# A decoder layer's start reordered, four unread matmuls added, and the last stage's loads, stores and final rows rewritten

## The chip, the cores and the metric

One core of a Trainium2 chip runs the whole program. The metric is the device time of one execution in microseconds. Engines are called as in the profile: PE (matmul), PEld (its weight loads), DVE, ACT, POOL, and the DMA queues of SP and POOL.

## The reference

The layer takes x (2048 x 1024, float32). Cut to what matters:

```python
h = rms_norm(x, pre_g)
q, k, v, g_ret, u, g_pool = split(h @ w_in, 6)            # 1024 -> 6 x 1024
y_ret = group_norm(retention(rope(q), rope(k), v)) * silu(g_ret)   # 8 heads, chunks of 128
y_pool = pooling(u, pool_w) * silu(g_pool)                # windows 2, 4, 8, 16
y = concat([y_ret, y_pool]) @ w_out                       # 2048 -> 1024
return x + rms_norm(y, post_g)
```

The rotary tables are the sine and cosine of position times inverse frequency.

## The kernel before

**The matmuls.** Every float32 matmul is made of three passes: both operands are split into a high part (ACT, `split`, L144) and a rest (DVE, L145), and high by high, high by rest and rest by high are accumulated (L330 to L332). The projections are done for pairs of 512-row blocks by Strassen's scheme in Winograd's form. A `Unit` has four quadrants, 11, 12, 21 and 22, of 128 x 512, and seven products of twelve matmuls each, in the order 6, 2, 5, 7, 1, 4, 3, where product 1 is that of the next unit. The scheme needs sums of quadrants: S1 = 21 + 22 and S3 = 11 + 21 are made while loading (`land`, L261 a plain load on SP's queue, then L263 a second load on POOL's queue that adds to the tile), S2 = S1 + 11 and S4 = S2 + 12 on DVE (L281). Four PSUM banks of the tag `acc` hold products; DVE takes results out of them (L313, L340, L348, L354, L693).

**The stages.** `first()` (written in a fixed order, which `manual_schedule` keeps) makes the statistics of x for blocks 0 and 1 and the first head without Strassen. Then four phases of units follow: mixer units of blocks 0 and 1, of blocks 2 and 3, and two of output units, eight each, over the two halves of the 2048 channels. In the phases a planner orders each engine's instructions; `later(i, f)` puts f into the i-th next slot, of which there is one per product.

**The start.** SP's queue issues row tile 0 of x (128 x 1024), the constants `cst`, the positions, row tiles 1 to 3, the gains `col`, then transposed x and weights. ACT squares each row tile in place with a sum (L862); DVE works out angles from the positions (`angles`, eight instructions at L835), six of them while it waits for the rows; then mean and inverse root (L370, L134 to L139), a diagonal (L376), which PE spreads over partitions (`rb`, L384), the rests of two weight tiles (L878) and the last two angle steps. The loop over `made((s11, s21))` is the first block: in each of eight rounds DVE scales a tile by `rb` (L932) and makes its rest (L940), ACT its high part (L936), DVE in most rounds the rest of a weight tile (L878), and PE does six matmuls (L951 to L953). The second block (k index 2 and 3) uses the same tiles, the third is the first one's for block 1, the fourth the second's; in the second DVE does block 1's angles and statistics and the rotary multiplications.

**The last phase.** Each of its eight output units adds the other phase's partial sums (`parts`, loaded at L687 into tiles of the tag `t`, of which there are 16), takes squares on ACT (L697) and then, in `finish`, an inverse root on DVE, four multiplications with the scale and the gain `pg` (L723), four DMAs on POOL's queue that add x to the tiles (L729), and four slots later four stores on SP's queue (L733). The very last unit (`final`) does each row when its two quadrants are there: x loaded at L722, multiplied at L723, three of four additions on POOL and one on DVE (L727), stored at L731.

Of the kernel before, what the change touches and what calls it, by code (L numbers as in the profile page):

```python
# [81 lines left out]
def layer_kernel(ctx: ExitStack, tc: tile.TileContext, x, xt, pos, wt, wut, wo, pw, cols, postg, const, out):  # L82
# [14 lines left out]
    cst = kp.tile([P, C_W], F32, name="cst")  # L97
    col = kp.tile([P, 3 * KT], F32, name="col")
# [153 lines left out]
    class Unit:  # L252
        def __init__(self, name, quads, uses):
            self.name, self.quads, self.uses = name, quads, uses
            self.op, self.bank = {}, {}
            self.fetch = self.part = None

# [8 lines left out]
        def load_sums(self):  # L266
            self.raw = {}
            self.land("S1", "21", "22")
            self.land("S3", "11", "21")

        def load_rest(self, names):
            for q in names:
                self.land(q, q)
# [15 lines left out]
        def prep(self, i):  # L289
            raw = self.raw  # L290
            if i == 1:
                h11 = raw["11"]
                self.split(1, "11")
                self.add("S2", raw["S1"], h11, nc.vector)
            elif i == 2:
                self.add("S4", raw["S2"], raw["12"], nc.vector)
                self.split(6, "S2")
            elif i == 3:
                self.split(2, "12")
            elif i == 4:  # L300
# [361 lines left out]
    def out_unit(s, f0, last, final=False):  # L662
# [21 lines left out]
        def fetch():  # L684
            for q in ("11", "22", "21", "12"):
                parts[q] = T(f"pt{q}_{n}")[:, :BLK]
                nc.sync.dma_start(out=parts[q], in_=place(part, q))  # L687

        def total(q):
            def use(c, i):  # L690
                t = o[q] = T(f"ot{q}_{n}")[:, :BLK]
                if i:
                    nc.vector.tensor_tensor(out=t, in0=c, in1=parts[q], op=ALU.add)  # L693
                else:
                    c(t)
                k = 2 * (int(q[0]) - 1) + int(q[1]) - 1
                nc.scalar.activation(out=parts[q], in_=t, func=AF.Square, scale=1.0 / 32.0,  # L697
                                     accum_out=s2[:, k:k + 1])
                if final and q == "21":
                    finish(("22", "21"))  # L700
                elif final and q == "12":
                    finish(("11", "12"))
                elif q == "12":
                    later(2, lambda: finish(("11", "22", "21", "12")))
            return use

        def finish(quads):
            k0, nr = int(quads[0][0]) - 1, len(quads) // 2
            rows_s = slice(0, 2) if nr == 2 else slice(k0, k0 + 1)
            v = sml.tile([P, nr], F32, name=f"ov{n}{k0}", tag=f"ov{nr}")  # L710
            s3 = s2.rearrange("p (s j) -> p s j", j=2)
            nc.vector.scalar_tensor_tensor(out=v, in0=s3[:, rows_s, 0], scalar=EPS, in1=s3[:, rows_s, 1],
                                           op0=ALU.add, op1=ALU.add)
            rs = rsqrt(v, nr, f"f{n}{k0}")
            for q in quads:
                k, j = (int(q[0]) - 1 if nr == 2 else 0), int(q[1]) - 1
                t = o[q]
                row = rows[q[0]]
                spot = (slice(row * P, (row + 1) * P), slice(j * BLK, (j + 1) * BLK))
                if final:  # L720
                    xr = T(f"xr{q}_{n}")[:, :BLK]
                    nc.sync.dma_start(out=xr, in_=x[spot])  # L722
                nc.vector.scalar_tensor_tensor(out=t, in0=t, scalar=rs[:, k:k + 1], in1=pg[j],  # L723
                                               op0=ALU.mult, op1=ALU.mult)
                if final:
                    eng = nc.vector if q == "12" else nc.gpsimd
                    eng.tensor_tensor(out=t, in0=t, in1=xr, op=ALU.add)  # L727
                else:
                    nc.gpsimd.dma_start(out=t, in_=x[spot], accum_op=ALU.add)  # L729
                if final:  # L730
                    nc.sync.dma_start(out=out[spot], in_=t)  # L731
                else:
                    later(4, lambda t=t, spot=spot: nc.sync.dma_start(out=out[spot], in_=t))  # L733

        u = Unit(n, quads, {q: total(q) for q in quads})
        u.fetch, u.part = fetch, parts
# [106 lines left out]
    def first():  # L843
# [63 lines left out]
        load_w(1, 0)  # L907
        load(b11[1], xt[0, 1])
# [90 lines left out]
        for i in made((s11, s21)):  # L999
# [9 lines left out]
            if i == 2:  # L1009
                trig(0)  # L1010
# [173 lines left out]
```

## Time and profile before

| | us |
|---|---|
| median of 3 runs | 1480.18 (1474.72 to 1480.51) |
| profiled execution, its own time | 1476.45 |
| span of the profile | 1474.5 |
| PE busy | 1423.2 (97%) |

The span runs from the first to the last instruction of the profiled execution. Times in rows are microseconds from its start.

### The profile page before, as it was taken

The page shows a single profiled execution, that of the slowest core. Times are in us where ns is not written, and L with a number is a line of the kernel's source. Part 1 is how long each engine was busy: PE and PEld are TensorE (multiplying, and loading weights), DVE is VectorE, ACT ScalarE, POOL GpSimd, SP SyncE. Part 2 cuts the span into 40 slices and gives each one's busy share as a digit, 9 for nine tenths or more (in the row PEclk, how much of TensorE's full clock was granted, in tenths as well). Part 3 has the DMA queues.
Part 4 walks back from the last instruction along what each step waited for, and adds up shares of the span by engine and source line. Part 5 has one row for each costly group of instructions (what it writes and reads, how often), then busy time and mean ns, then how long its engine had stood idle before and what let it go on. Part 6 is the DMA issues. An engine that isn't in the chain of part 4 may idle for free. (4 is left out here: it accounts for less than half of the span.)

```text
span 1474.5 us, 20756 instructions
## 1 busy us (share of the span) xinstructions
PE 1423.2 (97%) x6976; PEld 1188.4 (81%) x6976; DVE 1085.0 (74%) x2360; ACT 712.3 (48%) x1353; POOL 249.1 (17%) x335
## 2 busy tenths in 40 slices
PE   5999999999999999999999999999999999998985
PEld 3788888888888888888888888888888788877764
DVE  7997677878867788967787868687778544676665
ACT  6464565545554545745444444454446433553321
POOL 0001010211111222110111112111111222202222
PEclk9999999999999999999999999999999999999998
DMA  9135365635363768743535536444638755789976
GB/s 341 30 92 135 89 174 149 189 102 154 111 172 100 235 202 240 244 108 94 151 115 153 160 101 171 127 153 134 168 92 268 216 153 152 229 273 227 235 209 164
DMA packets 115370, 243.77 MB, mean 165 GB/s; under 512 B 14016, under 2 KB 14144, under 8 KB 115264
## 3 DMA queue, kind: packets, MB, share of 16 engines
q1 hardware_dynamic: 79296, 156.46, 32.1%
q0 software_dynamic: 35968, 86.00, 25.8%
q8 instruction: 54, 0.88, 0.3%
q14 instruction: 52, 0.43, 0.1%
HBM read 187.88 MB, written 54.53 MB: 164 GB/s over the span
## 5 line engine op out<-in xcount | busy, mean ns | idle before, releaser
L330 PE MATMUL b_o<-rh,h_o 128*128 128x512 f32 x192 | 76.3, 398 | 11.6 <-DVE ot_o L348 11.6
L331 PE MATMUL b_o<-rl,h_o 128*128 128x512 f32 x192 | 76.1, 396 | 0.7 <-DVE rl L145 0.7
L332 PE MATMUL b_o<-rh,l_o 128*128 128x512 f32 x192 | 76.0, 396 | 0.0
L330 PE MATMUL b_up<-rh,h_up 128*128 128x512 f32 x192 | 75.5, 393 | 0.0
L450 POOL DMA_DIRECT2D yd<-sg x32 | 24.1, 753 | 304.0 <-DVE sg L531 226.3
L332 PE MATMUL b_up<-rh,l_up 128*128 128x512 f32 x192 | 74.8, 390 | 0.0
L331 PE MATMUL b_up<-rl,h_up 128*128 128x512 f32 x192 | 74.8, 389 | 0.0
L330 PE MATMUL b_vg<-rh,h_vg 128*128 128x512 f32 x180 | 72.0, 400 | 0.0
L330 PE MATMUL b_qk<-rh,h_qk 128*128 128x512 f32 x180 | 71.2, 396 | 0.0
L332 PE MATMUL b_qk<-rh,l_qk 128*128 128x512 f32 x180 | 70.3, 391 | 0.1
L332 PE MATMUL b_vg<-rh,l_vg 128*128 128x512 f32 x180 | 70.4, 391 | 0.0
L331 PE MATMUL b_vg<-rl,h_vg 128*128 128x512 f32 x180 | 70.2, 390 | 0.0
L331 PE MATMUL b_qk<-rl,h_qk 128*128 128x512 f32 x180 | 70.2, 390 | 0.0
L524 ACT ACTIVATE on<-op,sh,y_o 128x128 f32<-128x128 f32 x128 | 48.2, 457 | 36.9 <-DVE sh L521 36.9
L145 DVE TENSOR_TENSOR rl<-m,rh 128x1024 fp32r<-128x1024 f32 x42 | 51.1, 1223 | 19.6 <-ACT rh L144 15.5
L263 POOL DMA_DIRECT2D S_qk<-in_wt x30 | 26.4, 907 | 170.4 <-DMA S_qk<-in_wt 119.3
L330 PEld LDWEIGHTS b_o<-rh,h_o 128*128 128x128 f32 x192 | 36.6, 191 | 21.6 <-DVE ot_o L348 13.6
L330 PE MATMUL a_o<-rh,h_o 128*128 128x512 f32 x128 | 49.9, 390 | 2.6 <-ACT x_o L338 2.6
L144 ACT CAST rh<-m 128x1024 fp32r<-128x1024 f32 x42 | 43.7, 1048 | 15.7 <-DMA m<-made 8.4
L330 PE MATMUL c_o<-rh,h_o 128*128 128x512 f32 x128 | 50.3, 393 | 0.8 <-ACT rh L144 0.8
L331 PE MATMUL c_o<-rl,h_o 128*128 128x512 f32 x128 | 50.1, 392 | 0.3 <-DVE rl L145 0.3
L332 PE MATMUL c_o<-rh,l_o 128*128 128x512 f32 x128 | 49.8, 389 | 0.0
(498 smaller groups left out, 4552.8 us busy)
## 6 DMA issues: line engine op xcount, KB each, us to landing
m<-made SPq DMA_DIRECT2D x30, 512.0 KB, 6.2
made<-c POOLq DMA_DIRECT2D x48, 256.0 KB, 3.8
yd<-sg POOLq DMA_DIRECT2D x32, 256.0 KB, 2.7
S_up<-in_wt POOLq DMA_DIRECT2D x32, 256.0 KB, 5.7
yd<-mx POOLq DMA_DIRECT2D x32, 256.0 KB, 3.1
b<-in_wo SPq DMA_DIRECT2D x32, 256.0 KB, 4.5
S_o<-yd SPq DMA_DIRECT2D x32, 256.0 KB, 3.0
S_o<-yd POOLq DMA_DIRECT2D x32, 256.0 KB, 7.5
```

The source lines that it names most:

```text
L144: nc.scalar.copy(out=r32(hi), in_=val)
L145: (eng or nc.vector).tensor_tensor(out=r32(lo), in0=val, in1=hi, op=ALU.subtract)
L263: nc.gpsimd.dma_start(out=dst, in_=self.quads[more], accum_op=ALU.add)
L330: nc.tensor.matmul(o, wh, mh, start=opens and j == 0, stop=False, **more)
L331: nc.tensor.matmul(o, wh, ml, start=False, stop=False, **more)
L332: nc.tensor.matmul(o, wl, mh, start=False, stop=j == KH - 1, **more)
L450: nc.gpsimd.dma_start(out=yd[b][:, :, f, :], in_=t.rearrange("p (c t) -> p c t", c=CPB))
L524: nc.scalar.activation(out=self.on[:, c], in_=op[:, c], func=AF.Identity, scale=rs[:, i:i + 1], bias=shift[:, i:i + 1])
```

## The change

At the start all four row tiles are loaded first, then `cst`, which now holds the gains as well (one DMA less); the positions come after the first weights. Four matmuls of `ones` with half a squared row tile each write a PSUM tile that nothing reads: three follow the squares of row tiles 0 to 2, the fourth stands behind `rb` on PE. The eight angle steps move: one behind the weight rests, six into the rounds 2 to 7 of the first block, one behind it. The rotary tables' sine and cosine (`trig(0)`, ACT) move from round 2 to behind the squares of block 1.

In the last phase the units are `plain`: quadrants 21 and 22 are loaded as they are, and S1 and S3 are made on DVE, two additions per unit, in place of three more loads, two of which add. `finish` begins one slot earlier and is spread over two slots; the stores go to POOL's queue, two slots after the DMA that adds x. In the final unit x is loaded together with the partial sums, each quadrant is multiplied by the gain as it arrives, and one DVE instruction per quadrant scales it and adds x.

```diff
-    cst = kp.tile([P, C_W], F32, name="cst")
-    col = kp.tile([P, 3 * KT], F32, name="col")
+    cst = kp.tile([P, C_W + 3 * KT], F32, name="cst")
+    col = cst[:, C_W:]
...
@@ Unit
         def load_sums(self):
             self.raw = {}
+            if self.plain:
+                self.land("21", "21")
+                self.land("22", "22")
+                return
             self.land("S1", "21", "22")
             self.land("S3", "11", "21")
 
         def load_rest(self, names):
             for q in names:
-                self.land(q, q)
+                if q not in self.raw:
+                    self.land(q, q)
...
         def prep(self, i):
             raw = self.raw
-            if i == 1:
+            if i == 0 and self.plain:
+                self.add("S1", raw["21"], raw["22"], nc.vector)
+            elif i == 1:
                 h11 = raw["11"]
+                if self.plain:
+                    self.add("S3", raw.pop("21"), h11, nc.vector)
                 self.split(1, "11")
                 self.add("S2", raw["S1"], h11, nc.vector)
...
@@ out_unit
             for q in ("11", "22", "21", "12"):
                 parts[q] = T(f"pt{q}_{n}")[:, :BLK]
                 nc.sync.dma_start(out=parts[q], in_=place(part, q))
+            if final:
+                for q in ("22", "21", "12", "11"):
+                    xr[q] = T(f"xr{q}_{n}")[:, :BLK]
+                    nc.sync.dma_start(out=xr[q], in_=x[spot(q)])
...
-                if final and q == "21":
-                    finish(("22", "21"))
-                elif final and q == "12":
-                    finish(("11", "12"))
+                if final:
+                    nc.vector.tensor_tensor(out=t, in0=t, in1=pg[int(q[1]) - 1], op=ALU.mult)
+                    if q in ("21", "12"):
+                        row = q[0]
+                        rs = scales(int(row) - 1, 1)
+                        for e in (row + "2", row + "1") if row == "1" else (row + "1", row + "2"):
+                            nc.vector.scalar_tensor_tensor(out=o[e], in0=o[e], scalar=rs, in1=xr[e],
+                                                           op0=ALU.mult, op1=ALU.add)
+                            nc.sync.dma_start(out=out[spot(e)], in_=o[e])
                 elif q == "12":
-                    later(2, lambda: finish(("11", "22", "21", "12")))
+                    later(1, finish)
...
+        def finish():
+            rs = scales(0, 2)
+
+            def normed(q):
+                k, t = int(q[0]) - 1, o[q]
                 nc.vector.scalar_tensor_tensor(out=t, in0=t, scalar=rs[:, k:k + 1], in1=pg[int(q[1]) - 1],
                                                op0=ALU.mult, op1=ALU.mult)
-                if final:
-                    eng = nc.vector if q == "12" else nc.gpsimd
-                    eng.tensor_tensor(out=t, in0=t, in1=xr, op=ALU.add)
-                else:
-                    nc.gpsimd.dma_start(out=t, in_=x[spot], accum_op=ALU.add)
-                if final:
-                    nc.sync.dma_start(out=out[spot], in_=t)
-                else:
-                    later(4, lambda t=t, spot=spot: nc.sync.dma_start(out=out[spot], in_=t))
+                nc.gpsimd.dma_start(out=t, in_=x[spot(q)], accum_op=ALU.add)
+                later(2, lambda: nc.gpsimd.dma_start(out=out[spot(q)], in_=t))
+            for i, q in enumerate(("11", "22", "21", "12")):
+                later(i // 2, lambda q=q: normed(q))
...
-        u.fetch, u.part = fetch, parts
+        u.fetch, u.part, u.plain = fetch, parts, True
...
@@ first
-        xs = {0: [row(0, 0)]}
+        xs = {0: [row(0, st) for st in range(CPB)]}
         nc.sync.dma_start(out=cst, in_=const)
-        load_pi(0)
-        xs[0] += [row(0, st) for st in range(1, CPB)]
-        nc.sync.dma_start(out=col, in_=cols)
...
         load_w(0, 0)
         load_w(1, 0)
+        load_pi(0)
         load(b11[1], xt[0, 1])
...
         turn = turns(0)
+        busy = rps("busy")
+
+        def keep_busy(t):
+
+            nc.tensor.matmul(busy, ones, t, start=True, stop=True)
         for st in range(CPB):
             square(0, st, xs[0][st])
-        for step in turn[:6]:
-            step()
+            if st < 3:
+                keep_busy(xs[0][st][:, :BLK])
         spread(0)
+        keep_busy(xs[0][3][:, :BLK])
         for k in (0, 1):
             split_w(k, 0)
             rest_w(k, 0)
-        for step in turn[6:]:
-            step()
+        turn.pop(0)()
...
             if i in upper:
                 split_w(*upper[i])
-            if i == 2:
-                trig(0)
+            if i >= 2:
+                turn.pop(0)()
+        turn.pop(0)()
...
         for st in range(CPB):
             square(1, st, xs[1][st])
+        trig(0)

```

## Rows read from the trace of the kernel before

**Rows 1.** The page, part 1: engine, busy us, share, instructions

```profile
PE 1423.2 (97%) x6976; PEld 1188.4 (81%) x6976; DVE 1085.0 (74%) x2360; ACT 712.3 (48%) x1353; POOL 249.1 (17%) x335
```

**Rows 2.** PE's waits, 1300 to 1460: us in total, times, longest

```profile
PE b_o L330 <- DVE ot_o L348: 11.6, 4, 4.5
PE a_o L330 <- ACT x_o L338: 2.6, 1, 2.6
```

**Rows 3.** Timeline, PE around 1352: start us, us, instruction

```profile
1351.02 0.63 PE L331 MATMUL b_o<-rl,h_o 128*128 128x512 f32 x1
1351.45 0.63 PE L332 MATMUL b_o<-rh,l_o 128*128 128x512 f32 x1
...
1353.73 0.40 PE L332 MATMUL b_o<-rh,l_o 128*128 128x512 f32 x1
1353.96 0.40 PE L330 MATMUL c_o<-rh,h_o 128*128 128x512 f32 x1
```

**Rows 4.** Windows: us; busy PE, PEld, DVE, ACT, POOL; granted clock; DMA share; GB/s

```profile
1350.00:1400.00 50.00, 49.06 (x210) 40.07 (x209) 33.01 (x74) 19.17 (x42) 11.27 (x13) 0.97 0.93 231
1400.00:1450.00 50.00, 43.85 (x185) 35.42 (x184) 32.33 (x75) 15.28 (x34) 11.83 (x14) 0.97 0.76 197
...
1459.50:1474.50 15.00, 0.00 (x0) 0.00 (x0) 9.58 (x25) 0.72 (x2) 4.57 (x3) 0.60 0.44 150
```

**Rows 5.** Groups of instructions, DVE, 1300 to 1460: busy us, mean ns, idle before

```profile
L281 DVE TENSOR_TENSOR sS_o<-S_o,11_o 128x512 f32<-128x512 f32 x6 | 4.1, 689 | 9.0 <-DMA S_o<-yd 9.0
```

**Rows 6.** SP's queue: whom it waited for, 1300 to 1460

```profile
SPq L733 <- DMA ot_o<-in_x: 70.2, 22, 13.9
SPq L261 <- DVE l_o L145: 18.2, 4, 6.2
```

**Rows 7.** Groups of instructions, POOL, 1300 to 1460

```profile
L729 POOL DMA_DIRECT2D ot_o<-in_x x28 | 24.6, 1073 | 79.7 <-DVE ot_o L723 79.7
```

**Rows 8.** Timeline, all engines, 0 to 20

```profile
2.12 1.39 SPq L853 DMA_DIRECT2D xs<-in_x  x3
...
9.15 0.43 DVE L835 TENSOR_SCALAR kk<-ang 128x512 f32<-128x512 f32 x1
...
10.07 2.14 DVE L835 SCALAR_TENSOR_TENSOR ang<-kk,ang 128x512 f32<-128x512 f32 x3
...
12.40 1.06 ACT L862 ACTIVATE xs<-xs 128x1024 f32<-128x1024 f32 x1 [0.15 <-DMA xs<-in_x]
...
13.58 0.17 DVE L370 TENSOR_SCALAR msf<-ss 128x4 f32<-128x4 f32 x1 [1.36 <-ACT xs L862]
...
16.50 2.08 PE L384 MATMUL rb<-dg,ones 128*128 128x512 f32 x2 [16.50 <-DVE dg L376]
...
18.63 1.40 DVE L932 SCALAR_TENSOR_TENSOR b<-b,col,rb 128x512 f32<-128x512 f32 x2
```

**Rows 9.** Timeline, PE's first products, 20 to 27

```profile
24.51 0.63 PE L952 MATMUL f<-b11h,wl 128*128 128x512 f32 x1
...
24.93 0.63 PE L953 MATMUL f<-b11l,wh 128*128 128x512 f32 x1
```

**Rows 10.** Windows of the first and the third block

```profile
18.60:32.45 13.85, 12.37 (x43) 9.98 (x44) 13.82 (x24) 11.05 (x20) 0.00 (x0) 1.00 1.03 404
...
42.48:54.06 11.58, 11.58 (x56) 9.59 (x55) 11.47 (x19) 5.61 (x10) 0.00 (x0) 1.00 0.00 1
```

**Rows 11.** PE's waits, 20 to 130

```profile
PE a_qk L332 <- DVE l_qk L145: 0.6, 1, 0.6
```

**Rows 12.** DMA view, 0 to 40: GB/s in slices of 1 us

```profile
GB/s 0 33 197 378 212 111 303 389 416 408 415 394 430 383 402 403 406 397 391 389 404 416 408 401 410 399 420 397 406 410 414 393 391 379 260 100 102 127 168 133
```

**Rows 13.** Timeline, the end, 1457 to 1476

```profile
1458.81 0.39 PE L332 MATMUL c_o<-rh,l_o 128*128 128x512 f32 x1
...
1462.84 1.22 DVE L138 TENSOR_TENSOR t_fo<-t_fo,y_fo 128x1 f32<-128x1 f32 x1
...
1467.93 1.64 DVE L727 TENSOR_TENSOR ot_o<-ot_o,xr_o 128x512 f32<-128x512 f32 x1
```

More of the change, by code (lines that the diff above doesn't have):

```diff
@@ L81, in layer_kernel @@
 @with_exitstack
-def layer_kernel(ctx: ExitStack, tc: tile.TileContext, x, xt, pos, wt, wut, wo, pw, cols, postg, const, out):
+def layer_kernel(ctx: ExitStack, tc: tile.TileContext, x, xt, pos, wt, wut, wo, pw, postg, const, out):
     nc = tc.nc
@@ L256, in __init__ @@
             self.fetch = self.part = None
+            self.plain = False
         def land(self, name, q, more=None):
@@ L703, in use, with spot, scales @@
                 elif q == "12":
-                    later(2, lambda: finish(("11", "22", "21", "12")))
+                    later(1, finish)
             return use
-        def finish(quads):
-            k0, nr = int(quads[0][0]) - 1, len(quads) // 2
-            rows_s = slice(0, 2) if nr == 2 else slice(k0, k0 + 1)
+        xr = {}
+        def spot(q):
+            row, j = rows[q[0]], int(q[1]) - 1
+            return slice(row * P, (row + 1) * P), slice(j * BLK, (j + 1) * BLK)
+        def scales(k0, nr):
@@ L710, in finish @@
             v = sml.tile([P, nr], F32, name=f"ov{n}{k0}", tag=f"ov{nr}")
             s3 = s2.rearrange("p (s j) -> p s j", j=2)
-            nc.vector.scalar_tensor_tensor(out=v, in0=s3[:, rows_s, 0], scalar=EPS, in1=s3[:, rows_s, 1],
+            nc.vector.scalar_tensor_tensor(out=v, in0=s3[:, k0:k0 + nr, 0], scalar=EPS, in1=s3[:, k0:k0 + nr, 1],
                                            op0=ALU.add, op1=ALU.add)
[L714 to L719, printed above, removed]
-                if final:
-                    xr = T(f"xr{q}_{n}")[:, :BLK]
-                    nc.sync.dma_start(out=xr, in_=x[spot])
-                nc.vector.scalar_tensor_tensor(out=t, in0=t, scalar=rs[:, k:k + 1], in1=pg[j],
-                                               op0=ALU.mult, op1=ALU.mult)
-                if final:
-                    eng = nc.vector if q == "12" else nc.gpsimd
-                    eng.tensor_tensor(out=t, in0=t, in1=xr, op=ALU.add)
-                else:
-                    nc.gpsimd.dma_start(out=t, in_=x[spot], accum_op=ALU.add)
-                if final:
-                    nc.sync.dma_start(out=out[spot], in_=t)
-                else:
-                    later(4, lambda t=t, spot=spot: nc.sync.dma_start(out=out[spot], in_=t))
@@ new lines, in scales @@
+            return rsqrt(v, nr, f"f{n}{k0}")
+        def finish():
+            rs = scales(0, 2)
+            def normed(q):
+                k, t = int(q[0]) - 1, o[q]
+                nc.vector.scalar_tensor_tensor(out=t, in0=t, scalar=rs[:, k:k + 1], in1=pg[int(q[1]) - 1],
+                                               op0=ALU.mult, op1=ALU.mult)
+                nc.gpsimd.dma_start(out=t, in_=x[spot(q)], accum_op=ALU.add)
+                later(2, lambda: nc.gpsimd.dma_start(out=out[spot(q)], in_=t))
+            for i, q in enumerate(("11", "22", "21", "12")):
+                later(i // 2, lambda q=q: normed(q))
@@ L1171 @@
         "wut": c(wut),
-        "wo": c(np.asarray(w_out).reshape(FT, P, DM)), "pw": c(pw), "cols": c(cols),
-        "postg": c(np.asarray(post_norm_g).reshape(1, DM)), "const": _constants(),
+        "wo": c(np.asarray(w_out).reshape(FT, P, DM)), "pw": c(pw),
+        "postg": c(np.asarray(post_norm_g).reshape(1, DM)), "const": c(np.concatenate([_constants(), cols], axis=1)),
     }
```

## The prediction

> **What bounds the kernel now.** I read the page first: PE is busy for 1423.2 of 1474.5 us [rows 1], so what can be won is where PE stands still or runs at half clock, and what lies ahead of its first and behind its last matmul. Then the waits of PE by stage, and for each the queue of the engine it waited for.
>
> In the last phase PE waits four times, 11.6 us in all, for DVE's L348 to empty a PSUM bank, and once 2.6 us for ACT at the change of phase [rows 2]. After two of those waits the pitch of its matmuls is 0.43 us in place of 0.23 [rows 3]: 1.2 GHz, not 2.4. The granted clock of 0.97 over two stretches of 50 us [rows 4] says what that costs: 2 x 0.03 x 50 = 3.0 us. DVE is late there, not full: it is busy for 33 of 50 us [rows 4], and its idle time before the addition that needs S1 is a wait for the DMA, 9.0 us over four of six [rows 5]. That DMA is late since SP's queue stands in front of L733's stores, which wait for the DMAs that add x, 70.2 us in 22 waits [rows 6], and the loads of the next unit stand behind them; the second, adding half of each sum moreover queues on POOL, which itself waits for L723 for 79.7 us [rows 7].
>
> At the start the chain is: last row of x at 12.40, its squares, DVE at 13.58, PE's `rb` at 16.50, the first scaled tile at 18.63 [rows 8]. From there DVE bounds: 13.82 of 13.85 us in the first block and 11.47 of 11.58 in the third [rows 10], and at 70 us PE still waits for DVE [rows 11]. PE's first products are at half clock (pitch 0.42 [rows 9], though the clock column says 1.00 [rows 10]), yet DVE, which does not stop, sets the block's length.
>
> At the end 10.8 us lie between PE's last matmul at 1458.81 and the end of the last addition at 1469.57 [rows 13]; storing and closing take the 4.9 us from there to 1474.5.
>
> **The change part by part.**
>
> *Rows earlier.* Rows 1 to 3 are issued two DMAs earlier, 2 x 1.39/3 = 0.93 us [rows 8], and 0.17 MB of constants and 0.26 MB of positions no longer move ahead of them: 0.43 MB at some 410 GB/s [rows 12] is 1.05 us. The slices from 4 to 6 us move only 212 and 111 GB/s [rows 12]; if that dip belongs to those two small-row loads, another 0.48 MB/410 = 1.2 us go. So 1.0 to 2.6 us; I take 1.7. The constants now arrive behind the rows but are needed only by the diagonal, 2.9 us less a multiply after the squares; the positions land behind the second weight tile, and DVE asks for them only behind two weight rests. Both are covered; uncovered, each us late is a us of the start.
>
> *Angle steps moved.* Before, six of eight ran while DVE waited for rows, and two while PE made `rb`. Now one is covered by `rb`; the other seven are in or right behind the first block, where DVE has 0.03 us free. Two small ones and the last at about 0.45 and four multiply-adds at 2.14/3 = 0.71 [rows 8]: 3 x 0.45 + 4 x 0.71 = 4.2 us on the engine that bounds. A wait of DVE for block 1's squares, 0.2, is absorbed. The fourth block needs nothing from DVE and PE could catch up there, but PE's wait at 70 us [rows 11] says that DVE is again last behind it. So the delay arrives whole. Bounds: 0, if DVE had hidden slack, and 4.2.
>
> *`trig(0)` later* I cost at nothing: by my estimate ACT, with four squares of 1.06 [rows 8] and three table instructions behind the first block, is done some 2 us before DVE's rotary multiplications, which stand behind five angle steps and block 1's statistics. That cover gone, it would be the table instructions' 2 us.
>
> *Four unread matmuls.* Each is like `rb`, 2.08 us at half clock [rows 8]. Three run while PE has nothing else. The fourth stands between `rb` and the first product, and holds that back by about 0.5 us if the clock is low; DVE is behind PE then, so it is hidden. What they may bring is clock: `rb` at full clock saves 1.0, of which 0.5 counts, since DVE is busy with weight rests and an angle step until then. The twelve products at the low pitch, 12 x 0.2 = 2.4 us, bring nothing where DVE sets the pace: a round has at least 0.7 + 0.6 + 0.6 + 0.7 us of DVE work against six matmuls x 0.43 = 2.6. I count half of the 0.5.
>
> The Trainium skill, TensorE: Matmul & The Clock Gate, section "Why this matters for your kernels", says to keep TensorE continuously busy to get out of half rate; rows 3 agree after a pause, and by the page the matmuls would be worth 2.4 + 0.5 us more than I count. No row here shows unread matmuls.
>
> Start: 4.2 - 0.2 - 1.7 - 0.3 = **+2.0** us; with the bounds of the rows and `rb`, +0.9 to +3.0.
>
> *Plain loads.* In eight units two loads and two adding loads go, and one plain load takes their place (21; 22 was loaded anyway): three times 256 KB less per unit. Added are 16 DVE additions of 0.69 [rows 5], 1.4 us per unit of 84 matmuls x 0.23 = 19 us; DVE has a third of its time free [rows 4], so they are hidden. Uncovered they would be 11 us.
>
> *Stores on POOL's queue, earlier.* SP keeps only loads, so the 70.2 us in front of L733 leave it. On POOL 28 stores wait behind 28 adding DMAs of 24.6 us in total [rows 7]; the store comes two slots (5.4 us) behind the addition, the next unit's adding DMAs four slots later, so that nothing that PE needs stands behind them. A buffer wait of SP for DVE's L145, 18.2 us in four [rows 6], remains possible: the tags keep their sizes. It now has no late DVE to cause it.
>
> The Trainium skill, DMA: Bandwidth & Descriptors, section "Issuing engines are not separate DMA queues", says that issuing from several engines saves only the time of the issue. By that alone moving the stores gives nothing; rows 6 show another effect, loads queued behind a store that waits, so trace and page do not meet in the same place.
>
> The four waits (11.6) and the low clock behind them (3.0) make 14.6; I take **-14.0**, leaving 0.6 for small restarts. Bounds: -7, half of them back in another form, and -17.2, with the 2.6 of ACT's wait.
>
> *Final rows.* DVE work behind PE's last matmul is now: two multiplications by the gain (1.2), taking the last product out (0.6), two chains of eleven small instructions at 0.2 (4.4), less 0.8 where they interleave, four fused ones (2.65): 8.05 in place of 10.8, **-2.7**. The chain's length is from 13.58 to 16.50 less a multiply of 0.69 [rows 5, 8]. Gone with POOL's additions is what a small DVE instruction next to them took, 1.22 [rows 13] against 0.17 [rows 8]. Bounds -1.5 (no interleaving, DVE waits for ACT's squares) and -4.
>
> **Sum.** +2.0 - 14.0 - 2.7 = -14.7: 1476.45 becomes 1461.8. The median shown is 3.7 above the profiled execution; with half of that added I predict **1463.5** us. A difference of 0.5%, 7.4 us, is about what can be told from no change.
>
> **The rivals.** (a) *Half of it returns.* POOL's queue now holds adding DMAs and stores, and in the tags `t` and `x` a load waits for a late release, as SP did for L145 [rows 6]. Half of the 14 stays: 1463.5 + 7 = 1470.5. For it: the DMA engines are at 0.93 and 0.76 [rows 4]. Against it: less is moved. (b) *The start gains.* The clock is full from the first product and DVE's pace is not what held PE; then rows and clock count, -2.5 in place of +2.0: 1459. Against it, 13.82 of 13.85 [rows 10]. It is the way that the page on TensorE would have it go. (c) *The change doesn't do what it says:* the loads are late because the DMA engines are full, not because of the queue; the four waits stay, +2.0 - 2.7 = -0.7: 1477.5. For it the share of 0.93 [rows 4], against it the 70.2 us [rows 6]. It is the way that the page on DMA would have it go. (d) *Slower:* DVE's in-order queue now stands on two loads per unit in place of one, and if 21 or 22 waits for a free `x` buffer until L145 frees one, as four loads did for 18.2/4 = 4.55 us each [rows 6], seven units wait 32 us in place of the 14.6: +17 - 0.7, with the median 1494.6. It decides from (14.6 + 0.7 + 7.4)/7 = 3.2 us per unit on. Against it: by my count ten to twelve of the thirteen such tiles live at a time, as before.
>
> **Chances.** Forecast 0.66, (a) 0.14, (b) 0.10, (c) 0.06, (d) 0.04. The range runs from (b) with the last phase's and the end's lower bounds, 1459 - 3.2 - 1.3 = 1454.5, so 1455, to (a) with the upper bounds of the start and the end, 1470.5 + 1.0 + 1.2 = 1472.7, and a little more for the median, 1474. Faster by over 0.5%: forecast, (b) and most of (a), 0.88; within: (c) and the rest, 0.08; slower: 0.04.
>
> **What would show it.** In the changed profile: DVE's L370 at about 11.9, the first scaled tile at 16.5 to 17; angle steps between L940 and L932 in the first block, PE with gaps there; PE's wait at 70 us some 2 us later. In the last phase no wait of PE for L348, granted clock 1.00, SP without waits for DMAs that add. Behind the last matmul about 13 us to the end of the span, not 15.7. Wrong it would be if PE's waits move to other DVE lines in the last phase, or if the start's delay is absorbed by 100 us.

## The result, and the profile after

The changed kernel takes 1461.79 us (median of 4 runs, 1458.21 to 1464.46), the kernel before 1479.55 beside it: ratio 0.9883, 95% interval 0.9858 to 0.9909. A second set of runs of the same kernel gave 1458.84 and 0.9864 (0.9840 to 0.9889). Predicted were 1463.5 us, 1455 to 1474. The profiled execution took 1461.03 us, its span 1459.1, so 15.4 us less span than before; the prediction's sum was -14.7.

Where the 15.4 us came from is read by taking the same instruction in both traces and noting how much earlier or later it starts after the change:

| place | before | after | shift |
|---|---|---|---|
| first instruction of the statistics (L370, now L380) | 13.58 | 10.05 | -3.5 |
| first scaled tile (L932, now L946) | 18.63 | 14.44 | -4.2 |
| third matmul of the first Strassen product (`a_qk`) | 70.51 | 69.58 | -0.9 |
| PE near 300, from 620 to 1100, from 1170 to 1290 | | | -1.35, +0.15, +3.45 |
| PE's last matmul | 1458.81 | 1447.68 | -11.1 |
| end of the last DVE instruction | 1469.57 | 1456.06 | -13.5 |
| end of the span | 1474.5 | 1459.1 | -15.4 |

So the start won 0.9 us where a loss of 2.0 was predicted; 4.4 us were lost at two changes of phase in the middle, which the prediction did not foresee; the last phase gave -11.1 - 3.45 = -14.6 (predicted -14.0); and what lies behind the last matmul -4.3 (predicted -2.7). Together -0.9 + 4.4 - 14.6 - 4.3 = -15.4.

Page, part 1 of the changed kernel, beside [rows 1]:

```profile
PE 1427.4 (98%) x6984; PEld 1187.3 (81%) x6984; DVE 1091.3 (75%) x2379; ACT 714.5 (49%) x1353; POOL 245.9 (17%) x344
```

Timeline of the changed kernel, 0 to 20: start us, us, instruction, and idle time before it with its releaser; beside [rows 8, 9]:

```profile
0.74 1.81 SPq L869 DMA_DIRECT2D xs<-in_x  x4
...
4.33 1.06 ACT L878 ACTIVATE xs<-xs 128x1024 f32<-128x1024 f32 x1 [2.10 <-DMA xs<-in_x]
...
5.53 5.35 PE L1004 MATMUL busy<-xs,ones 128*128 128x512 f32 x6 [5.53 <-ACT xs L878]
...
8.87 1.06 ACT L878 ACTIVATE xs<-xs 128x1024 f32<-128x1024 f32 x1 [0.18 <-DMA xs<-in_x]
...
10.05 0.17 DVE L380 TENSOR_SCALAR msf<-ss 128x4 f32<-128x4 f32 x1 [8.82 <-ACT xs L878]
...
12.98 1.12 PE L394 MATMUL rb<-dg,ones 128*128 128x512 f32 x2 [2.10 <-DVE dg L386]
...
14.44 1.40 DVE L946 SCALAR_TENSOR_TENSOR b<-b,cst,rb 128x512 f32<-128x512 f32 x2
...
16.48 0.63 PE L966 MATMUL f<-b11h,wl 128*128 128x512 f32 x1
...
16.91 0.63 PE L967 MATMUL f<-b11l,wh 128*128 128x512 f32 x1
...
17.62 0.40 PE L966 MATMUL f<-b11h,wl 128*128 128x512 f32 x1
17.86 0.40 PE L967 MATMUL f<-b11l,wh 128*128 128x512 f32 x1
```

The four rows are issued in one go and the last lands 3.5 us earlier. PE has run three of the unread matmuls by then (six instructions, two for each), and `rb` runs in 1.12 us, not 2.08. PE's products show a pitch of 0.43 only up to 17.3, then 0.23. In the second profile of the same kernel (after_again) they are at the full clock from the first one on. DVE is what did not follow, as the next two views show: the windows of the whole first and of the third block (busy PE, PEld, DVE, ACT, POOL, then the clock, as in [rows 4]; beside [rows 10]) and PE's waits from 16 to 130 us (us in total, times, longest; beside [rows 11]).

```profile
14.44:31.79 17.35, 14.99 (x53) 9.60 (x51) 17.29 (x30) 10.90 (x19) 0.00 (x0) 0.91 1.03 406
...
41.54:53.00 11.46, 11.46 (x57) 9.37 (x56) 11.34 (x19) 5.49 (x9) 0.00 (x0) 1.00 0.00 1
```

```profile
PE a_qk L342 <- DVE l_qk L145: 1.8, 1, 1.8
PE f L967 <- DVE b21l L954: 1.6, 2, 0.8
```

DVE is busy for 17.29 of the 17.35 us that the first block now takes, 3.5 us more than before, since six of the seven angle steps stand in it and the last right behind it. From the third block's first scaled tile to the third matmul of the first Strassen product it takes 69.58 - 41.54 = 28.04 us; before it was 70.51 - 42.48 = 28.03. The faster PE only waits longer there: 1.8 in place of 0.6.

DMA view, 0 to 40, GB/s in slices of 1 us, beside [rows 12]:

```profile
GB/s 0 45 233 377 389 332 438 374 427 399 385 252 346 383 369 410 414 399 404 414 414 401 410 414 406 401 410 401 410 418 387 389 387 346 115 98 156 129 156 21
```

The dip of 212 and 111 in the slices from 4 to 6 us is gone (389 and 332).

The last phase: PE's waits from 1285 to 1450, the windows beside [rows 4], SP's waits and POOL's groups from 1300 to 1460 beside [rows 6, 7].

```profile
PE c_o L340 <- DVE x_o L323: 1.9, 1, 1.9
PE a_o L340 <- ACT x_o L348: 1.4, 1, 1.4
```

```profile
1350.00:1400.00 50.00, 50.00 (x222) 41.41 (x221) 41.28 (x94) 19.35 (x40) 15.19 (x22) 1.00 0.81 232
1400.00:1445.00 45.00, 41.52 (x181) 33.41 (x180) 29.13 (x64) 14.29 (x31) 13.52 (x19) 1.00 0.71 173
```

```profile
SPq L697 <- ACT pt_o L711: 19.5, 10, 3.8
SPq L262 <- PE b_o L342: 13.7, 5, 5.4
...
SPq L697 <- DMA ot_o<-in_x: 6.3, 1, 6.3
```

```profile
L746 POOL DMA_DIRECT2D ot_o<-in_x x28 | 24.7, 1013 | 71.1 <-DVE ot_o L744 66.6 <-ACT h_o L144 3.1 <-DVE x_o L323 0.7
L747 POOL DMA_DIRECT2D out<-ot_o x28 | 15.5, 555 | 45.0 <-DMA ot_o<-in_x 42.7 <-issue 2.3
```

No wait for L358 (before L348) is left, the others make 3.3 us, the clock is 1.00, and DVE is busy for 41 of 50 us in place of 33 without holding PE. SP's 70.2 us for adding DMAs are one wait of 6.3; 42.7 us of that kind now stand on POOL, in front of its stores. What SP's loads wait for now is mostly ACT and PE giving buffers back: they are early. PE is not wholly free of POOL's stores, as the waits of all engines from 1415 to 1446 show:

```profile
ACT x_o L348 <- DMA out<-ot_o: 5.8, 1, 5.8
DVE ot_o L707 <- DMA out<-ot_o: 5.8, 1, 5.8
```

Both need a tile that a store on POOL's queue still reads. PE's wait of 1.4 for that very ACT instruction follows from it, and probably the 1.9 for DVE's L323 ten microseconds later, up to which DVE has no idle time above 0.8. All eight profiles of kernels with the plain loads and the moved stores have these waits: 5.0 to 6.3 us for ACT and DVE, then 0.7 to 1.9 of PE for ACT and 1.9 for L323. They are most of what is left of PE's waits in the last phase.

The end, timeline from 1447, beside [rows 13]:

```profile
1447.68 0.39 PE L342 MATMUL c_o<-rh,l_o 128*128 128x512 f32 x1
...
1451.96 1.42 DVE L719 SCALAR_TENSOR_TENSOR ot_o<-ot_o,y_fo,xr_o 128x512 f32<-128x512 f32 x2
...
1454.65 1.41 DVE L719 SCALAR_TENSOR_TENSOR ot_o<-ot_o,y_fo,xr_o 128x512 f32<-128x512 f32 x2
```

From the last matmul's start to the end of DVE's last fused instruction are 8.38 us (1454.65 + 1.41 - 1447.68), before 10.76; from there to the end of the span 3.04, before 4.96. The last store lands 2.1 to 2.2 us behind DVE's end in both, so nearly all of the difference lies behind the last landing: 1.0 us to the end of the span, before 2.8. There the closing lines of the program drain each engine; POOL's drains before and after (number, then shortest/median/longest in ns, first and last start):

```profile
L1180 POOLq DRAIN  x3: 46/93/6422, 1467.3 to 1474.3; - x3
```

```profile
L1201 POOLq DRAIN  x3: 51/108/2831, 1448.5 to 1458.8; - x3
```

Before, POOL makes the last additions of x, and the drain behind them ends at 1473.8, 4.7 us after the last of these and 2.0 after the last store has landed. Now POOL has no addition there, and its drain is over by 1451.3. The five profiles in which POOL makes those additions have 2.8 us (plain_only 4.5) from the last landing to the end, the nine others 0.9 to 1.0. Why the drain lasts that long is not shown.

### The profile page after: what moved, and what is told of

Its sections match the earlier page's. It is cut to its first block, busy times and chain, and to the rows that moved or that the text cites. A ratio compares the mean times of both kernels' runs of the same rounds, so it can differ in the third digit from the quotient of the medians.

```text
span 1459.1 us, 20742 instructions
## 1 busy us (share of the span) xinstructions
PE 1427.4 (98%) x6984; PEld 1187.3 (81%) x6984; DVE 1091.3 (75%) x2379; ACT 714.5 (49%) x1353; POOL 245.9 (17%) x344
## 4 chain that ended last, share of the span: by engine, by line
PE 86%; DVE 6%; DMA 4%; issue 2%; ACT 1%; SPq 0%; DVEq 0%; POOLq 0%; ACTq 0%
PE b_vg L342 3%; PE b_vg L340 3%; PE b_vg L341 3%; PE b_up L341 3%; PE b_up L340 3%; PE b_up L342 3%; PE b_qk L342 3%; PE b_qk L341 3%; PE b_qk L340 3%; PE b_o L341 3%; PE b_o L340 3%; PE b_o L342 3%; PE op L514 2%; PE a_up L340 2%; PE a_up L341 2%; PE a_up L342 2%
## 5 line engine op out<-in xcount | busy, mean ns | idle before, releaser
L341 PE MATMUL b_vg<-rl,h_vg 128*128 128x512 f32 x180 | 70.2, 390 | 0.0
L145 DVE TENSOR_TENSOR rl<-m,rh 128x1024 fp32r<-128x1024 f32 x42 | 51.1, 1222 | 18.2 <-ACT rh L144 13.8
L144 ACT CAST h_o<-sS_o 128x512 fp32r<-128x512 f32 x48 | 29.7, 621 | 54.2 <-PE c_o L341 14.8
```

Of the source, the lines that this page charges most:

```text
L144: nc.scalar.copy(out=r32(hi), in_=val)
L145: (eng or nc.vector).tensor_tensor(out=r32(lo), in0=val, in1=hi, op=ALU.subtract)
L341: nc.tensor.matmul(o, wh, ml, start=False, stop=False, **more)
```

## The experiments

Thirteen profiles (after_again and no_matmuls_again repeat a kernel); "late at 1290" is how much later than before PE is when the last phase begins, "last phase" how much it gains or loses from there to its last matmul, "behind" what lies from the last matmul to the end of the span (15.72 before). Ratios are to runs of the kernel before on the same chip.

| kernel | ratio (95%) | `a_qk` | late at 1290 | last phase | behind |
|---|---|---|---|---|---|
| changed | 0.9883 (0.9858 to 0.9909) | 69.58 | +3.45 | -14.6 | 11.4 |
| start_only | 1.0010 (0.9995 to 1.0026) | 69.52 | +1.6 | +0.3 | 15.7 |
| last_only | 0.9879 (0.9864 to 0.9895) | 70.42 | -0.5 | -12.3 | 10.8 |
| plain_only | 0.9934 (0.9912 to 0.9956) | 70.57 | -1.2 | -10.6 | 17.5 |
| noplain | 0.9977 (0.9966 to 0.9988) | 70.64 | -0.3 | +3.7 | 11.8 |
| no_matmuls | 0.9864 (0.9843 to 0.9884) | 69.87 | -0.1 | -13.3 | 10.9 |
| matmuls_only | 1.0000 (0.9987 to 1.0013) | 70.54 | +3.0 | +1.9 | 15.7 |
| angles_late | one run, 1479.25 | 74.08 | +3.3 | -0.3 | 15.7 |
| angles_early | 0.9858 (0.9842 to 0.9875) | 68.92 | +1.2 | -15.1 | 12.2 |
| best | 0.9852 (0.9827 to 0.9876) | 68.49 | -1.6 | -12.3 | 10.9 |
| after_again | 0.9864 (0.9840 to 0.9889) | 69.27 | +1.3 | -13.1 | 10.9 |
| no_matmuls_again | 0.9862 (0.9838 to 0.9886) | 70.32 | +1.1 | -14.1 | 12.2 |
| one_small | 0.9860 (0.9835 to 0.9884) | 69.82 | 0.0 | -14.9 | 11.6 |

**start_only and last_only: the two halves of the change.** The first has the kernel before with the new start (all of the diff in `first`, and `col` inside `cst`), the second the diff in `Unit` and `out_unit` on the old start. Of their diffs to the kernel before:

```diff
@@ start_only @@
+        xs = {0: [row(0, st) for st in range(CPB)]}
...
+                keep_busy(xs[0][st][:, :BLK])
...
+        turn.pop(0)()
@@ last_only @@
+                later(2, lambda: nc.gpsimd.dma_start(out=out[spot(q)], in_=t))
...
+        u.fetch, u.part, u.plain = fetch, parts, True
```

> The start of the change alone; the last phase is the kernel before's. Theory A (the rows come 3.5 us earlier and the spread matmul runs at full clock, against seven angle steps of 3.3 us on a full DVE): by 82 us the changed kernel is 0.9 us ahead, PE waits four times for L348 in the last phase as before (about 12 us), 1478 us, ratio 0.998 to 1.001. Rival B (the start also causes the 4.4 us that the changed kernel loses at the two changes of phase near 590 and 1150 us): the same losses show here, and the time is 3 to 4 us above the kernel before, ratio 1.002 to 1.003. If they do not show, they belong to one execution's DMA times or to the planner's order with the new last phase.

> The new last phase and final unit on the kernel before's start. Theory A: no wait of PE for L348, granted clock 1.00 from 1300 us on, 14 to 15 us less between the start of the last phase and PE's last matmul, 4 us less behind it: 18 us less in all, about 1461, ratio 0.987 to 0.989. Rival (the gain needs the earlier start, or part of it came from there): under 14 us less, ratio over 0.990.

The start alone moves nothing in the time (1.001), though its `a_qk` is 1.0 us earlier; its profile loses that and 1.6 us more in the middle, 2.6 in all where the rival had 4.4; the new last phase alone gives all of it (0.9879 against 0.9883 and 0.9864 for the whole; theory A had 0.987 to 0.989, with 14 to 15 us in the last phase where 12.3 were measured). The gain lies in the last phase and the end.

**plain_only and noplain: which part of the last phase.** plain_only keeps `finish` and the stores on SP as before and has only the plain loads with DVE's two additions:

```diff
-        u.fetch, u.part = fetch, parts
+        u.fetch, u.part, u.plain = fetch, parts, True
```

noplain has everything else of the last phase (stores on POOL's queue, `finish` spread out, the new final unit) and loads the sums with adding DMAs as before:

```diff
-        u.fetch, u.part, u.plain = fetch, parts, True
+        u.fetch, u.part = fetch, parts
```

> Only the plain loads of 21 and 22 with S1 and S3 on DVE; finish, stores on SP's queue and the final unit are the kernel before's. Theory A (SP's queue, where the next unit's loads stand behind stores that wait, is a cause of its own): half of the 14.6 us or less is won, PE still waits 4 to 9 us for L348, SP still waits some 60 us or more at the stores; about 1472, ratio 0.994 to 0.997. Rival C (the adding loads on POOL were the cause, and by the Trainium skill, DMA: Bandwidth & Descriptors, moving stores to another queue gives only issue time): all 14 us are won here, about 1465, ratio 0.990.

> Stores on POOL's queue, the staged finish and the new final unit, but S1 and S3 are made by adding loads as in the kernel before. Theory A: SP is free, but the adding loads queue on POOL behind stores that wait for the DMAs that add x; the DVE addition that needs S1 still waits for the DMA, PE waits 4 to 9 us; with the end's 4.3 us about 1468 to 1470, ratio 0.991 to 0.994. Rival C: no gain in the last phase but the end's 4.3, about 1475, ratio 0.997.

plain_only, PE's waits and SP's:

```profile
PE b_o L340 <- DVE ot_o L358: 4.3, 2, 2.2
```

```profile
SPq L743 <- DMA ot_o<-in_x: 69.2, 22, 9.4
```

DVE's wait for its first addition, that of S1, from 1300 to 1460 in plain_only (group of instructions: busy us, mean ns, idle before):

```profile
L287 DVE TENSOR_TENSOR sS_o<-21_o,22_o 128x512 f32<-128x512 f32 x6 | 4.1, 686 | 6.0 <-DMA 22_o<-yd 6.0
```

noplain, PE's waits, SP's, and DVE's group that takes S1:

```profile
PE b_o L340 <- DVE ot_o L358: 10.6, 4, 3.8
PE a_o L340 <- ACT x_o L348: 3.4, 1, 3.4
```

```profile
SPq L262 <- DVE l_o L145: 44.7, 14, 12.1
```

```profile
L287 DVE TENSOR_TENSOR sS_o<-S_o,11_o 128x512 f32<-128x512 f32 x6 | 4.1, 690 | 17.4 <-DMA S_o<-yd 17.4
```

And the same group in the changed kernel:

```profile
L287 DVE TENSOR_TENSOR sS_o<-21_o,22_o 128x512 f32<-128x512 f32 x6 | 4.1, 688 | 1.0 <-DMA 22_o<-yd 0.9
```

How the sum travels, from 1300 to 1460: the loads of S1 and S3 (number, size, median us from issue to landing) before, where the half on POOL's queue is issued once the half on SP's has landed,

```profile
S_o<-yd SPq DMA_DIRECT2D x12, 256.0 KB, 5.2
S_o<-yd POOLq DMA_DIRECT2D x12, 256.0 KB, 8.3
```

and in plain_only, where the two quadrants of S1 travel side by side:

```profile
21_o<-yd SPq DMA_DIRECT2D x6, 256.0 KB, 4.6
22_o<-yd SPq DMA_DIRECT2D x6, 256.0 KB, 4.3
```

From the issue of the first half of S1 to the landing of the second are 14.1 us before (mean of six), 15.5 in noplain, 5.9 in plain_only and 7.8 in the changed kernel. The idle time of DVE in front of S1 orders the four kernels: 17.4 us (noplain, last phase +3.7), 9.0 (before), 6.0 (plain_only, -10.6), 1.0 (changed, -14.6). Taking the stores off SP while the sums are still added by DMA gives nothing: SP's wait at the stores is gone, but its loads now wait for a free buffer of L145 (18.2 us in four before, 44.7 in fourteen now), S1 is later than before and PE's waits for L358 stay, at 10.6 us where theory A had 4 to 9. That does not price SP's queue alone: in noplain the stores stand on POOL's queue in front of the adding halves, and POOL waits there for 32.9 us in 20 for the DMAs that add x. No run has the sums added by DMA and the stores on a third queue. The Trainium skill, DMA: Bandwidth & Descriptors, section "Issuing engines are not separate DMA queues", says that spreading the issue over engines saves only issue time. For the stores alone noplain agrees: its last phase is 3.7 us longer, not shorter.

The plain loads do most of it alone, with SP's 69.2 us of waiting at L743 still there: 10.6 us, where theory A had half of the 14.6 at most and the rival all of it. What they change is two things at once, the second transfer that waits for the first, and three loads of 256 KB fewer per unit; the runs do not take these apart, but a single load needs nearly as long with them (4.3 to 4.6 us) as before (5.2). With the moved stores as well, S1's wait falls from 6.0 to 1.0 and the last two waits for L358 go, in all eight profiles; the last phase gains another 1.7 to 4.5 us (-12.3 to -15.1), 1.7 of it on the old start, where only one profile of each kernel stands against the other. plain_only's 17.5 us behind the last matmul, 1.7 more than before, are due to POOL's drain, which ends 3.4 us after the last store has landed. What noplain does gain, ratio 0.9977 (rival C had 0.997), is the end: 11.8 us behind the last matmul in place of 15.7.

**no_matmuls, matmuls_only: the four unread matmuls.** The first is the changed kernel without `busy`, the second the kernel before with it:

```diff
+            if st < 3:
+                keep_busy(xs[0][st][:, :BLK])
         spread(0)
+        keep_busy(xs[0][3][:, :BLK])
```

> The changed kernel without its four unread matmuls. Theory A (the four matmuls only bring the spread matmul to full clock): it takes 2.1 us again instead of 1.1, the first scaled tile comes 0.6 us later than the changed kernel's 14.44, PE's first dozen products run at half clock, but DVE sets the pace of the first block: the third matmul of the first Strassen product starts 0.6 us later than the 69.6 of the changed kernel, about 70.2. Rival B (the clock counts, as the Trainium skill, TensorE: Matmul & The Clock Gate, would have it): the low clock of the first dozen products adds 2.4 us as well, 72.5 or later. The time itself cannot tell them apart: 1460 to 1464, ratio 0.987 to 0.991.

> The kernel before with the four unread matmuls alone. Theory A: the spread matmul takes 1.1 us instead of 2.1, but DVE is busy until 18.6 with weight rests and angle steps, so the first scaled tile stays at 18.6; PE's first products run at full clock, the third matmul of the first Strassen product stays within 0.3 us of 70.5; ratio 1.000, 0.998 to 1.002. Rival B: it comes 2 to 3 us earlier.

`rb` in no_matmuls and in matmuls_only:

```profile
12.64 2.08 PE L394 MATMUL rb<-dg,ones 128*128 128x512 f32 x2 [12.64 <-DVE dg L386]
```

```profile
16.55 2.07 PE L384 MATMUL rb<-dg,ones 128*128 128x512 f32 x2 [1.71 <-DVE dg L376]
```

Without the matmuls `rb` is back at 2.08 us, the first scaled tile at 14.75 in place of 14.44, and `a_qk` at 69.87 in place of 69.58. In this execution the rows landed 0.3 us earlier (L380 at 9.71, not 10.05); counted from L380, `a_qk` comes after 59.5 to 59.6 us in the three profiles with the matmuls and the change's start, and after 60.2 in the three without (one_small among them). So the matmuls are worth 0.6 to 0.7 us at `a_qk`, the 0.6 that theory A had, and all of it is `rb`: PE's products stay at the low clock until 21.9, but DVE sets the pace. In matmuls_only they buy nothing at all (18.68, 70.54). There PE idles for 1.71 us between the third of them and `rb`, and `rb` takes 2.07, against my expectation; in the changed kernel it idles for 2.10 before the `rb` that takes 1.12. In angles_early they precede `rb` too, PE idles for 2.25, and `rb` takes 2.07. What differs is not settled by these profiles.

**angles_late, angles_early: the price of the moved angle steps.** angles_late is the kernel before with only the angle steps and `trig(0)` moved as in the change. angles_early is the changed kernel with the positions and constants loaded first and all eight steps in front of the first statistics; its diff to the changed kernel:

```diff
+        load_pi(0)
+        nc.sync.dma_start(out=cst, in_=const)
         xs = {0: [row(0, st) for st in range(CPB)]}
-        nc.sync.dma_start(out=cst, in_=const)
...
+        for step in turn:
+            step()
...
-            if i >= 2:
-                turn.pop(0)()
```

and of angles_late to the kernel before:

```diff
-        for step in turn[:6]:
-            step()
...
-            if i == 2:
-                trig(0)
+            if i >= 2:
+                turn.pop(0)()
```

> The kernel before with only the angle steps and the sine and cosine moved as in the change. Theory A (seven steps on a DVE that is full cost 3.3 us): the first scaled tile stays near 18.6, the first scaled tile of block 1 comes at 45.7 in place of 42.5, the third matmul of the first Strassen product at 73.8 in place of 70.5. Rival (DVE has slack that takes the steps): within 1 us of 70.5. Time about 1480.

> The changed kernel with positions and constants loaded ahead of the rows and all eight angle steps in DVE's idle time before the rows are there. Theory A (the rows are 1.05 us later by 0.43 MB at 410 GB/s, the 3.3 us of angle steps leave the full stretch of DVE): the mean at about 11.1, the first scaled tile at about 15.2, the third matmul of the first Strassen product at 67.0 to 67.5 in place of 69.6; 2 us less than the changed kernel, about 1459 to 1460, ratio 0.986 to 0.988. Rival (the dip of the DMA between 4 and 6 us comes back with those two loads in front): rows 2.3 us later and the product at 68.5; no gain that can be measured.

In angles_late the first scaled tile comes at 18.93 (+0.3) and `a_qk` at 74.08 (+3.6): the steps cost 3.3 us, and the delay is still there at 1286. In the changed kernel they cost the same: from the first scaled tile to `a_qk` the shift goes from -4.19 to -0.93, 3.26 us; in no_matmuls from -3.88 to -0.64, 3.24. That is net: the first block is 3.53 longer (17.35 to 13.82), and a wait of DVE for block 1's squares, which the delay absorbs, gives 0.27 back. The prediction had 4.2 and 0.2. Its 0.71 for a step is from three in a row that each need the last one's result; between other work the next instruction starts 0.60 behind it:

```profile
28.92 0.69 DVE L851 SCALAR_TENSOR_TENSOR ang<-kk,ang 128x512 f32<-128x512 f32 x1
29.52 0.69 DVE L954 TENSOR_TENSOR b21l<-b,b21h 128x512 fp32r<-128x512 f32 x1
```

In angles_early the first scaled tile comes at 16.75, not at 15.2 as expected: the rows now come behind the positions and constants (statistics at 11.72, not 10.05), and `rb` takes 2.07 again, unread matmuls or not; `a_qk` is earlier than in the changed kernel by 0.66, not by 2. What the steps gain (3.0), the later rows (1.7) and the slow `rb` (0.7) take for the most part; the rival, rows 2.3 us later and the product at 68.5, is nearer than theory A.

**best, after_again, no_matmuls_again, one_small: what the profiles could not settle alone.** After eight experiments PE had lost 1.8 to 3.3 us behind a change of phase near 1150 in all four profiles with the unread matmuls, and in none of five without. To tell whether they cost this, the changed kernel and the one without them ran once more, beside angles_early without them (best) and the change with one small unread matmul (one_small):

```diff
+        nc.tensor.matmul(busy[:, :P], ones, ones, start=True, stop=True)
         spread(0)
```

> The change without the four unread matmuls, with the positions and constants loaded first and all eight angle steps in front of the first statistics. Theory A (VectorE sets the pace at the start, and the unread matmuls cost 2 to 3 us near 1150): third matmul of the first Strassen product near 69 us, as in the kernel with the matmuls, waits near 1150 no longer than 1.2 us, time 1453 to 1456, ratio 0.983 to 0.985. Theory B (the loss near 1150 is a matter of one execution, not of the matmuls): the same start, and the time as that of the kernel with the matmuls and early angles, 1457, ratio 0.9855 to 0.9865.

> The changed kernel once more, for a second profile and more times. If the loss near 1150 belongs to the kernel: TensorE waits there again 2.1 to 2.3 us for a weight half whose load lands late, and the start of its last matmul is near 1447.5; the ratio is 0.987 to 0.989. If it belongs to one execution: the wait is under 1.2 us and the last matmul starts near 1445.

> The change without the four unread matmuls once more. If they cost time later on: no wait above 1.2 us near 1150, and the ratio again 0.002 or more below that of the changed kernel run beside it (0.985 to 0.987). If not: the two ratios agree within 0.001.

> The change with one unread matmul of 128 columns of ones in place of the four. If the extra PSUM tile of the rotation sets the loss near 1150: the wait of 2.1 to 2.3 us there is back, and the time is that of the changed kernel. If the count of matmuls sets it, or nothing does: the wait is under 1.2 us, and the time is that of the kernel without them, with rb's matmuls still slow (2.0 us).

PE's waits from 1140 to 1200 in the changed kernel's first profile,

```profile
PE c_o L340 <- ACT rh L144: 2.3, 1, 2.3
```

and in its second:

```profile
PE b_o L341 <- DVE rl L145: 1.1, 2, 0.8
PE c_o L341 <- DVE rl L145: 0.3, 1, 0.3
```

The same kernel waits there for 2.3 us in one execution and not at all for the same half of a weight in another. ACT, which makes that half, waits for its load from `wo` for 4.0 us in the first and for 1.8 in the second: the transfer landed later. So 2.4 of the 3.3 us that the first profile loses near 1150 belong to the execution; the second loses 1.0 there, and the three new ones without the four matmuls 0.4 or less. By their times the kernels with and without the matmuls, run side by side, are alike (0.9864 and 0.9862), and matmuls_only is at 1.0000; but these intervals leave room for some 2 us. The profiles do not clear the matmuls: from `a_qk` to 1290 the five with all four of them lose 2.6 to 4.4 us against the kernel before, the eight others 1.2 at most. one_small, with the additional PSUM tile but one small matmul, is among the eight (0.7 us, `rb` at 2.08), so the tile alone is not the cause. Whether the four matmuls cost time later on stays open. after_again falls between its two expectations: no wait above 1.2 us near 1150, but the last matmul at 1447.1, near the 1447.5 of the first of them.

best, with `a_qk` 2.0 us before that of the kernel before, has the lowest ratio, 0.9852, but its interval holds those of the changed kernel: 2 us of 1460 can't be told here.

## Why the prediction was right, step by step

*Start, +2.0 predicted, -0.9 measured at 70 us:* the terms were right in kind, and three of the four mis-sized. Rows earlier: I took 1.7, with 1.0 to 2.6 as bounds; it was 3.5. The parts that I had named, 0.93, 1.05 and 1.2, add up to 3.2, and I took half of that; the dip in [rows 12], which I had left open, did belong to the two small-row loads. Angle steps: I took 4.2 from durations in [rows 8]; the first block grew by 3.5, and 0.3 were absorbed where I had 0.2. `rb` gave 0.66 (4.19 - 3.53) where I counted 0.3. So 3.53 - 0.27 - 3.53 - 0.66 = -0.93. The mechanism held: DVE bounds the first blocks, the delay of moved DVE work arrives whole, and PE's full clock for the products is not worth 2.4 us there. My sign that PE's wait at 70 us comes 2 us later was wrong by the sizes.

By its number the start is nearer to rival (b), -2.5, than to my +2.0, but not by its cause: the rows did it, not the clock. PE's products had the low clock up to 17.3 in one profile of the changed kernel and not at all in the other, and in no_matmuls up to 21.9, with `a_qk` 0.6 to 0.7 us apart, which `rb` explains. The Trainium skill, TensorE: Matmul & The Clock Gate, section "Why this matters for your kernels", says to keep the engine continuously busy to get out of half rate. The trace agrees that the clock comes up that way (pitch 0.23 from 17.6 on); what it does not show is a gain for the products, since they wait for DVE.

*Middle, nothing predicted, +4.4 in the profile:* not seen. The second profile of the same kernel lost 2.6 (from -1.24 at `a_qk` to +1.34 at 1290), so some 1.8 of the 4.4 belong to the execution; some 1.5 near 600 are in both profiles. The cause of what recurs stays open.

*Last phase, -14.0 predicted, -14.6 measured* (-12.3 to -15.1 over the eight profiles of kernels that have both parts): the size is right, and the four waits and the low clock went as stated. It was worked out from PE's waits and clock alone and would have held for whatever cause the change removed. But the cause that I named first, SP's queue in front of L733's stores, is the smaller part. I read the 70.2 us [rows 6] as what makes S1 late; plain_only leaves these 70 us and gains 10.6, noplain takes them away and gains nothing, though there the stores stand in front of the adding halves. What made S1 late for the most part was that its second half is an adding DMA that starts when the first has landed, 8.3 us behind 5.2, which I had only as "moreover". Rival (c) had the four waits stay, and they went; its reason, full DMA engines, is not excluded as a part, since the plain loads also move less.

*Final rows, -2.7 predicted, -4.3 measured:* up to DVE's last instruction 10.76 became 8.38, -2.4, close to the 8.05 that I had added up (7.8 to 9.2 over the nine profiles with the new final unit). The other 1.9 lie between DVE's end and the end of the span (4.96 to 3.04). I had left them as they were; they were POOL's drain behind the additions that the change takes from it.

*Sum:* -14.7 predicted, -15.4 in the profile, in which errors of -2.9, +4.4, -0.6 and -1.6 stand against each other. That the sum came so close is luck; that the gain lies in the last phase and the end is not. The median came lower than the predicted time by 1.7 in the one set and 4.7 in the other.

Rival (d) did not come: SP's wait for L145 fell from 18.2 to 5.4 us. Of rival (a), a late release behind POOL's stores, a small part came: PE's 1.4 us, and probably the 1.9 for L323, and waits at another DVE line were a sign of being wrong. I had reckoned that nothing that PE needs stands behind those stores; the tiles that they read do.

## What to carry to other kernels

A long wait in a queue is not yet the cause of what is late behind it: look at which arrival the bound engine's producer waits for (here DVE for S1), and which step of that transfer ends last. A sum that is fetched by a plain and then an adding transfer lands a whole transfer later (8.3 us here); where an engine has a third of its time free, two plain loads and its own addition (0.69 us) can be worth far more than the addition costs. Work moved onto the engine that bounds a stretch is paid in full, by the time from its start to the next instruction's (0.60 us here) and not by its duration in a dependent chain (0.71). A faster clock of an engine that waits there for the bound one brought nothing here. And look at what keeps the program open behind its last store: here an engine's drain, 1.8 us.

## What the runs showed of the hardware beyond that

The clock after a pause can differ from execution to execution. In two profiles of the kernel without the matmuls PE waits 1.8 us for the same instruction. PE's timeline in the first (no_matmuls)

```profile
69.87 0.50 PE L342 MATMUL a_qk<-b11h,l_qk 128*128 128x512 f32 x1 [1.75 <-DVE l_qk L145]
70.20 0.39 PE L340 MATMUL a_qk<-b11h,h_qk 128*128 128x512 f32 x1
70.44 0.39 PE L341 MATMUL a_qk<-b11l,h_qk 128*128 128x512 f32 x1
```

and in the second (no_matmuls_again):

```profile
70.32 0.50 PE L342 MATMUL a_qk<-b11h,l_qk 128*128 128x512 f32 x1 [1.81 <-DVE l_qk L145]
...
70.92 0.63 PE L341 MATMUL a_qk<-b11l,h_qk 128*128 128x512 f32 x1
71.35 0.63 PE L342 MATMUL a_qk<-b11h,l_qk 128*128 128x512 f32 x1
...
74.30 0.39 PE L340 MATMUL b_qk<-rh,h_qk 128*128 128x512 f32 x1
74.53 0.40 PE L341 MATMUL b_qk<-rl,h_qk 128*128 128x512 f32 x1
```

In the first the pitch is 0.23 right away (2.4 GHz), in the second 0.43 up to 74.3 (1.2 GHz, granted clock 0.76 over the stretch from 69 to 76): 1.6 us lost from the same wait. Together with a load that ACT waits 2.2 us longer for in one execution (4.0 against 1.8, above), it means that single profiles of one kernel can differ by some 2 us at the same place, so that a difference of this size between one profile each does not tell two kernels apart.
